# Residual rounds and the gating of the last weights beside the middle chunks of the second products; differences of u from the float32 blocks

## The chip, the core and the metric

One core of one Trainium2 chip runs the whole program. The time is device time of one execution, in microseconds; a kernel's time is the median of its runs. The work is matrix products on TensorE (PE), with VectorE (DVE), ScalarE (ACT) and GpSimd (POOL) preparing operands and taking results, and with DMA transfers, most of them issued from SyncE's queue (SP).

## The reference, cut to what matters

Input x is 1024 tokens of width 1024. Two blocks with adaptive modulation (an even mixer and attention, each followed by an MLP) are followed by a third block with a gated feed-forward network (ffn). The lines that bear on the change:

```
x = layer_norm(ALPHA * x + gate * y, ln_g[layer, 0], ln_b[layer, 0])     # y: the mixer's output
u = x * (1.0 + scale) + shift
y = square(relu(u @ mlp_w1 + mlp_b1)) @ mlp_w2 + mlp_b2                  # 1024 -> 4096 -> 1024
x = layer_norm(ALPHA * x + gate * y, ln_g[layer, 1], ln_b[layer, 1])
...
x = _layernorm(DEEPNORM_ALPHA * x + mix, ln1_g, ln1_b)                   # third block
ffn = (silu(gate half) * value half of conv(x @ w_up)) @ w_down          # 1024 -> 2 x 2816 -> 1024
x = _layernorm(DEEPNORM_ALPHA * x + ffn, ln2_g, ln2_b)
```

The residual of each such pair is ALPHA times the normalised x with the layer norm's scale and bias, plus the bias b2 times the gate in the MLPs. The gate multiplies a whole column of y, so it can be put on the product's result or on the rows of w2.

## The kernel before

All operands of TensorE are pairs of a rounded part and its float32 remainder: ACT casts (`act.copy`), DVE subtracts, and a product is three matmuls (hi x hi, hi x lo, lo x hi). Helpers issue most vector work, so that many instructions stand on one line: `tt` (L305) and `stt` (L308) on DVE, or on POOL when asked; the matmuls all stand on L247.

**Boundary** (`boundary`, L575). Between two parts of the network the last rows of the product before are finished, the rows are normalised into `xres` (z: the normalised rows without scale and bias), and `u_tile` (L567) makes transposed tiles of u: TensorE transposes (L251), ACT writes scale and shift into a float32 tile `uf` (L571), ACT casts it to u's high part (L572), DVE subtracts for the low part. u has two halves of tokens h = 0, 1 and eight tiles of channels. The rows z go to `d_zm` in DRAM.

**First products** (`FmProducts`). u times w1 (or w_up) is done in a scheme with seven products for a 2 x 2 division, instead of eight, on 14 pairs of weight blocks in an MLP and 20 in the ffn. A group is one of the seven, 12 matmuls. It needs differences of blocks: of the weights (`wx`, in part on POOL, and `we`, cast and split), and of u: `diffs` makes the operands `t` for one of four channel positions each time two tiles of the second half are there. It adds u's high and low parts back together (`ur<-u`, on POOL for the first half, on DVE for the second), takes four differences (`tx`, `ur`), casts and splits. Results gather in `rr` (MLP) or `cc` (ffn), the ffn's convolution runs on `cc` and `rr`, and `keep_pair` stores h and its differences (`hx`) in DRAM.

**Residual rounds** (`residual_job`). For each of eight row tiles: load z from `d_zm` into `zt`, `zt` x ALPHA x scale on DVE, + bias row on POOL, store to `d_zm`. The rows stand in `xrow` and `erow`, loaded from POOL's queue. It is a generator; `bg()` runs one step of it at every odd group of the first products.

**Second products** (`second_half`, `TmProducts`). h times w2 goes by the same kind of scheme in chunks of 4, 3, 3, 4 pairs (MLP) or 3, 3, 3 (ffn); a chunk has seven groups g and each group four steps t of 3 matmuls per pair. `he` are the split operands (from `rh`, loads of h, and from `rw`, weights), `beside` and `fetch` make and load them for the groups ahead. Sums go into `acc`, rows of the result, by DVE. In the MLPs the first touch of `acc` is a copy by ACT; in the ffn `acc` is loaded with the residual from `d_zm` ahead. In the last chunk of an MLP `gated_residual` multiplies `acc` by the gate on POOL and adds `zi`, loaded from `d_zm`. The first MLP's second products also carry `ada_side`, the modulation of later parts. The last four pairs of rows of w2 (`wl`) are handled apart, by the boundary after (`last_sums`); since `acc` is already multiplied by then, `wl` is multiplied by the gate: `_Weights.gate` on POOL (L194), `st<-st,gate`, ahead of the split.

**What sets the order.** Each engine runs its instructions in the order of the program. Tiles come from rotating pools: W8 (8 KB a partition, 21 tiles) and T4 (4 KB, 7 tiles: `sf`, `wx`, `rh`, `zt`, `zi`, `uf`, `tx`, `ur`, `gate`, `erow`). SP issues a load once a tile is free, and a store once what it stores is ready; what stands behind waits.

Of the kernel before, what the change touches and what calls it, by code (L numbers as in the profile page):

```python
# [254 lines left out]
def tile_net(ctx: ExitStack, tc: tile.TileContext, x, wts, ada, adag, cols, rows, sfm, rgw, wup, wsp, out):  # L255
# [66 lines left out]
    d_f = drm.tile([16, 4, 1024], F32, name="d_f")  # L322
    d_h = drm.tile([14, 7, 128, 512], F32, name="d_h")
    d_hx = drm.tile([4, 128, 1024], F32, name="d_hx")
    d_zm = drm.tile([1024, 1024], F32, name="d_zm")
# [71 lines left out]

    def last_plan(l, name, first, gate):

        for j in range(4):  # L400
            plan.append({"src": (lambda j=j: d_hx[j]), "mix": ("h", l, j)})
        for j in range(4):
            plan.append({"key": (name, first + j), "dst": lambda: W8("wl")})
            if gate is not None:
                plan[-1]["gate"] = gate

    def mlp_plan(l):
        W(f"w1_{l}", 0, 1, 2, 3)
        last_plan(l, f"w2_{l}", 28, lambda: gate_row.get(2 * l + 1))

# [25 lines left out]
    W("up", 0, 22, 1, 23)  # L436
    last_plan(2, "dn", 18, None)
    ws = _Weights(k, plan)
# [126 lines left out]

    def u_tile(xz, h, kt, uT, G, B, lo=None):
        pb = PB()  # L567
        for j in range(4):
            pe.transpose(pb[:, j * 128:(j + 1) * 128], xz[:, 4 * h + j, kt * 128:(kt + 1) * 128], ident)
        uf = T4("uf")[:, 0:512]  # L570
        act.activation(out=uf, in_=pb, func=AF.Identity, scale=G[:, kt:kt + 1], bias=B[:, kt:kt + 1])  # L571
        act.copy(uT[h][:, 0, kt, :], uf)  # L572
        tt(uT[h][:, 1, kt, :], uf, uT[h][:, 0, kt, :].bitcast(F32), SUB, lo)

    def boundary(hs, wsx, xres, G, B, keys, evacs, spill=None, ops=None):  # L575
# [5 lines left out]
        def residual(t):  # L581

            if spill is not None:
                xr = xres[:, t, :]
                stt(xr, xr, spill[1], rr[0], MUL, MUL)
                tt(xr, xr, rr[1], ADD, None if t % 2 else pool)
                nc.sync.dma_start(out=spill[0][t * 128:(t + 1) * 128, :], in_=xr)
            elif ops is not None:
                nc.sync.dma_start(out=d_zm[t * 128:(t + 1) * 128, :], in_=xres[:, t, :])
        for t in range(8):  # L590
# [4 lines left out]
            for dh in range(2):  # L595
                if t >= 5:
                    for _ in range({(5, 0): 2, (6, 0): 2}.get((t, dh), 1)):
                        u_tile(xres, 0, todo.pop(0), uT, G, B)
                if dh == 0 and norm:
# [26 lines left out]
        for i in (1, 2):  # L626
            w.append(ws.get(keys[i], ahead=0))
            for c, _ in enumerate(fm_mms(pss[i], w[i], uT, 0)):
                if c in (1, 5):
                    residual(2 * i - 2 + c // 4)  # L630
                if (i, c) in ((1, 3), (1, 5), (1, 7), (2, 0), (2, 2), (2, 3), (2, 5), (2, 6)):
                    u_tile(xres, 1, todo.pop(0), uT, G, B)
                    if ops is not None and len(todo) % 2 == 0:
                        diffs(uT, 3 - len(todo) // 2, ops)
        for c, _ in enumerate(fm_mms(pss[0], w[0], uT, 1)):
# [854 lines left out]
    def residual_job(alpha, gname, bname, extra):  # L1490

        if extra is not None:
            load_gate(extra[1])
        gr, cr = xrows(alpha, gname, bname, extra)
        if extra is not None:
            del gate_row[extra[1]]
        yield
        for t in range(8):
# [66 lines left out]
    class Mlp:  # L1565
# [20 lines left out]
        def run(self, uT, jobs=None):  # L1586
# [35 lines left out]

            bgq.append(residual_job(ALPHA, f"lng{2 * l}", f"lnb{2 * l}", (f"b2_{l}", 2 * l + 1)))
# [11 lines left out]
            undefer(9)  # L1635
            return second_half(l, tp, 2 * l + 1, jobs)

# [20 lines left out]

    def second_half(l, tp, gate, jobs=None):

        xres = Rows("acc")
        if gate is None:
            for i in range(4):
                nc.sync.dma_start(out=xres.t[i], in_=d_zm[i * 256:(i + 1) * 256, :].rearrange("(i p) n -> p i n", p=128))
        else:
            load_gate(gate)
            if jobs:
                bgq.append(ada_side(jobs, 1, lambda: st.j in (0, 5, 6)))

        def step(g, t):  # L1670
            c, j = divmod(g, 7)
            st.j = j
            if jobs:
                bg()
# [5 lines left out]
        bg(99)  # L1680
        if gate is not None:
            gated_residual(xres, gate, 1, 0)
        hs, w2 = tail_blocks()
# [590 lines left out]
    def ffn(bargs):  # L2274
# [60 lines left out]

        bgq.append(residual_job(ALPHA2, "ln1g", "ln1b", None))

        def step(p, i):
            undefer()
            if p < fp.n - 1:  # L2340
                if i % 2:
                    bg()
            else:
                begin(tp, i)
# [3 lines left out]
        undefer(9)  # L2348
        return second_half(2, tp, None)

# [94 lines left out]
```

## Time and profile before

| | us |
|---|---|
| median of 3 runs (lowest, highest) | 3838.15 (3836.57, 3841.23) |
| the profiled execution; its span | 3834.72; 3833.0 |
| busy: PE, DVE, ACT, POOL | 3554.3, 2751.7, 1460.0, 715.9 |
| first products: MLP, second MLP, ffn | 293.77, 292.26, 430.10 |
| second products: MLP, second MLP, ffn | 291.99, 291.82, 188.06 |

The profiled execution is one run of the program, recorded by the hardware. A busy TensorE is not yet one at full clock: the granted clock stands beside the busy time of a stretch. A wait in square brackets is the idle time of an engine ahead of an instruction and what ended it.

### The profile page before, as it was taken

The numbers are of one execution on the slowest core, as the hardware profiler recorded it, in microseconds if no ns is written. First come the engines' busy times: TensorE is split into PE (matmuls) and PEld (weight loads), VectorE is DVE, ScalarE is ACT, GpSimd is POOL, SyncE is SP. The second block draws the span as 40 slices with busy tenths as digits, with TensorE's granted clock in tenths as the row PEclk, the third lists the DMA queues.
The fourth block names the chain that finished last, engine by engine and source line by source line (L and its number), as shares of the span: only waits on it lengthen the run. The fifth ranks groups of instructions, "written<-read, shape, count | busy, mean of one in ns | idle before, by whom it ended". The sixth has DMA issues, their size and how long they took to land. (4 is left out here: it accounts for less than half of the span.)

```text
span 3833.0 us, 43642 instructions
## 1 busy us (share of the span) xinstructions
PE 3554.3 (93%) x17098; PEld 2890.7 (75%) x17098; DVE 2751.7 (72%) x3609; ACT 1460.0 (38%) x1924; POOL 715.9 (19%) x473
## 2 busy tenths in 40 slices
PE   7999979999989999999897999998989988899997
PEld 5876767787867788878786778886777766677785
DVE  6565667768897764454556876688889678877787
ACT  4244343344325442353334334432423443344441
POOL 2002133400042000000202441004300034433002
PEclk9999989999999999999899999999989999999998
DMA  6333135465432222100312455344212223322641
GB/s 221 105 132 129 75 118 191 174 231 195 162 122 95 68 79 86 35 34 29 110 72 104 179 181 213 130 165 138 80 57 79 84 82 118 127 99 80 220 150 67
DMA packets 181056, 461.82 MB, mean 120 GB/s; under 512 B 15313, under 2 KB 20065, under 8 KB 180850
## 3 DMA queue, kind: packets, MB, share of 16 engines
q1 hardware_dynamic: 173986, 437.96, 32.3%
q0 software_dynamic: 6864, 21.08, 1.6%
q8 instruction: 134, 2.20, 0.2%
q14 instruction: 72, 0.59, 0.0%
HBM read 337.85 MB, written 121.13 MB: 120 GB/s over the span
## 5 line engine op out<-in xcount | busy, mean ns | idle before, releaser
L247 PE MATMUL ps<-u,wu 128*128 128x512 f32 x2880 | 763.5, 411 | 23.6 <-ACT u L572 14.6
L247 PEld LDWEIGHTS ps<-u,wu 128*128 128x128 f32 x2880 | 538.7, 194 | 152.1 <-ACT u L572 15.8
L247 PE MATMUL ps<-he 128*128 128x512 f32 x2442 | 587.0, 400 | 33.3 <-DVE he L305 24.6
L247 PEld LDWEIGHTS ps<-he 128*128 128x128 f32 x2442 | 465.6, 191 | 147.3 <-DVE he L305 30.7
L247 PE MATMUL ps<-t,we 128*128 128x512 f32 x1728 | 435.6, 402 | 46.4 <-DVE cc L305 31.5
L247 PEld LDWEIGHTS ps<-t,we 128*128 128x128 f32 x1728 | 330.7, 193 | 130.9 <-DVE cc L305 37.1
L247 PE MATMUL pb<-u,we 128*128 128x512 f32 x1152 | 287.0, 398 | 16.1 <-ACT rr L1606 16.1
L247 PE MATMUL ps<-wu,u 128*128 128x256 f32 x1920 | 261.5, 290 | 15.1 <-DVE wu L218 13.0
L247 PEld LDWEIGHTS pb<-u,we 128*128 128x128 f32 x1152 | 219.4, 191 | 69.1 <-ACT rr L1606 18.7
L247 PEld LDWEIGHTS ps<-wu,u 128*128 128x128 f32 x1920 | 242.4, 193 | 25.8 <-DVE wu L218 13.6
L1432 ACT CAST he<-rw 128x1024 fp32r<-128x1024 f32 (+1 forms) x154 | 133.2, 910 | 293.0 <-DVE rw L305 275.9
L305 DVE TENSOR_TENSOR we<-sf,we 128x512 fp32r<-128x512 f32 x192 | 175.7, 926 | 92.4 <-ACT we L1325 90.0
L247 PE MATMUL ps<-pw,wu 128*128 128x512 f32 x816 | 211.0, 407 | 13.8 <-DVE xres L308 7.9
L1904 DVE TENSOR_REDUCE mx<-ps 128x1 f32<-128x128 f32 (+7 forms) x128 | 95.5, 754 | 172.5 <-PE ps L247 172.2
L305 DVE TENSOR_TENSOR acc<-acc,ps 128x1024 f32<-128x1024 f32 (+1 forms) x155 | 162.7, 1050 | 75.1 <-PE ps L247 67.7
L305 DVE TENSOR_TENSOR he<-rw,he 128x1024 fp32r<-128x1024 f32 (+1 forms) x154 | 168.3, 1134 | 45.3 <-ACT he L1432 45.3
L1944 ACT ACTIVATE p<-ps 128x1024 f32<-128x1024 f32 (+7 forms) x128 | 82.9, 649 | 303.5 <-PE ps L247 287.9
L247 PEld LDWEIGHTS ps<-pw,wu 128*128 128x128 f32 x816 | 155.2, 194 | 50.6 <-DVE xres L308 8.4
L305 DVE TENSOR_TENSOR he<-rh,he 128x1024 fp32r<-128x1024 f32 (+1 forms) x154 | 174.4, 1133 | 19.8 <-ACT he L1432 19.8
L1432 ACT CAST he<-rh 128x1024 fp32r<-128x1024 f32 (+1 forms) x154 | 135.5, 910 | 68.7 <-DMA rh<-d_h 37.2
L247 PE MATMUL pb<-he 128*128 128x512 f32 x666 | 159.6, 394 | 0.0
L1325 ACT CAST we<-wx 128x512 fp32r<-128x512 f32 x144 | 84.8, 619 | 188.3 <-POOL wx L305 138.1
(394 smaller groups left out, 6086.0 us busy)
## 6 DMA issues: line engine op xcount, KB each, us to landing
st<-in_wts_dram SPq DMA_DIRECT2D x116, 512.0 KB, 3.3
rh<-d_h SPq DMA_DIRECT2D x105, 512.0 KB, 5.4
sf<-in_wts_dram SPq DMA_DIRECT2D x96, 512.0 KB, 6.9
d_h<-hx SPq DMA_DIRECT2D x37, 1024.0 KB, 4.8
d_h<-rr SPq DMA_DIRECT2D x111, 256.0 KB, 2.3
sta<-in_ada_dram SPq DMA_DIRECT2D x48, 512.0 KB, 3.4
rw<-in_wts_dram SPq DMA_DIRECT2D x28, 768.0 KB, 4.6
sta<-in_adag_dram SPq DMA_DIRECT2D x32, 512.0 KB, 3.9
```

Of the source, the lines that this page charges most:

```text
L247: return self.eng.matmul(out=out, lhsT=lhsT, rhs=rhs, **kw)
L305: (eng or dve).tensor_tensor(out=o, in0=a, in1=b, op=op)
L1325: act.copy(d[:, 0, :], src)
L1432: act.copy(d[:, 0, 0:n, :], src)
L1904: dve.tensor_reduce(out=mx[:, t:t + 1], in_=ps[:, 0:n], axis=AX.X, op=ALU.max)
L1944: act.activation(out=p[:, 128 * i:1024], in_=ps[:, 128 * i:1024], func=AF.Exp)
```

## The change

`diffs` takes its blocks from the float32 tiles that ACT writes: `u_tile` is handed a tile to write, in W8 for the first half and in T4 for the second, and the sums `ur<-u` are no longer made. The casts and subtractions of `t` are four of 512 instead of two of 1024. The rows z go to `d_zm` where each is normalised. The residual rounds move from the first products into the second products, from g = 3 on: a step after every t in the first MLP, where the modulation's side work goes ahead of it, and after every other t elsewhere; what is left is done at the end of the chunk before the last. Both steps of a round are on DVE. The last weights of the MLPs are gated in the same place, by DVE, through DRAM (`d_wl`), and loaded gated in the last chunk. In the ffn `acc` is no longer loaded ahead; its residual is added in the last chunk as in the MLPs, without a gate.

```
-    def u_tile(xz, h, kt, uT, G, B, lo=None):
+    def u_tile(xz, h, kt, uT, G, B, lo=None, uf=None):
-        uf = T4("uf")[:, 0:512]
+        if uf is None:
+            uf = T4("uf")[:, 0:512]
...
             def z(t=t, y=y, nb=nb):
                 act.activation(out=xres[:, t, :], in_=xres[:, t, :], func=AF.Identity, scale=y, bias=nb)
+                if ops is not None:
+                    nc.sync.dma_start(out=d_zm[t * 128:(t + 1) * 128, :], in_=xres[:, t, :])
...
-    def diffs(uT, j, ops):
+    def diffs(b, ops):
-        raw = []
-        for h in range(2):
-            r = T4("ur")
-            for i in range(2):
-                q = uT[h][:, :, j + 4 * i, :]
-                tt(r[:, i * 512:(i + 1) * 512], q[:, 0, :].bitcast(F32), q[:, 1, :].bitcast(F32), ADD, pool if h == 0 else None)
-            raw.append(r)
-        (b11, b21), (b12, b22) = [(r[:, 0:512], r[:, 512:1024]) for r in raw]
+        (b11, b21), (b12, b22) = b
...
-        for d, r in zip(t, (x, raw[0])):
-            f = d.rearrange("p a b c -> p a (b c)")
-            act.copy(f[:, 0, :], r)
-            tt(f[:, 1, :], r, f[:, 0, :].bitcast(F32), SUB)
+        for i, q in enumerate(((x[:, 0:512], x[:, 512:1024]), (b11, b21))):
+            for j in range(2):
+                act.copy(t[i][:, 0, j, :], q[j])
+                tt(t[i][:, 1, j, :], q[j], t[i][:, 0, j, :].bitcast(F32), SUB)
...
             stt(z, z, alpha, gr, MUL, MUL)
-            tt(z, z, cr, ADD, pool)
+            tt(z, z, cr, ADD)
...
-    def gated_residual(xres, gate, th, dh):
+    def add_residual(xres, gate, th, dh):
...
-            tt(x, x, gate_row[gate][:, f].unsqueeze(1).to_broadcast([128, 2, 512]), MUL, pool)
+            if gate is not None:
+                tt(x, x, gate_row[gate][:, f].unsqueeze(1).to_broadcast([128, 2, 512]), MUL, pool)
             tt(x, x, z, ADD)
...
-                if p < fp.n - 1:
-                    if i % 2:
-                        bg()
-                else:
+                if p == fp.n - 1:
                     begin(tp, i)
...
-            for i in range(4):
-                nc.sync.dma_start(out=xres.t[i], in_=d_zm[i * 256:(i + 1) * 256, :].rearrange("(i p) n -> p i n", p=128))
...
+        def gated():
+            for j in range(4):
+                z = T4("zw")
+                nc.sync.dma_start(out=z, in_=wts[_UNITS[f"w2_{l}", 28 + j]])
+                yield
+                tt(z, z, gate_row[gate], MUL)
+                yield
+                nc.sync.dma_start(out=d_wl[j], in_=z)
+                st.written.add(("w", l, j))
+        def work():
             if jobs:
-                bgq.append(ada_side(jobs, 1, lambda: st.j in (0, 5, 6)))
+                yield from ada_side(jobs, 1, lambda: st.j in (0, 5, 6))
+            yield from job
+            if gate is not None:
+                yield from gated()
...
+            if g > 2 and (jobs or t % 2 == 0):
+                next(side_work, None)
             if g >= tp.n - 7:
-                if gate is not None and t == 3 and j in (2, 5, 6):
-                    gated_residual(xres, gate, *((0, 0), (0, 1), (1, 1))[(2, 5, 6).index(j)])
+                if t == 3 and j in (2, 5, 6):
+                    add_residual(xres, gate, *((0, 0), (0, 1), (1, 1))[(2, 5, 6).index(j)])
...
+            elif g == tp.n - 8 and t == 3:
+                run(side_work)
...
-        tp = TmProducts("dn", [[0, 1, 2], [3, 4, 5], [6, 7, 8]], False)
+        tp = TmProducts("dn", [[0, 1, 2], [3, 4, 5], [6, 7, 8]], True)
```

DVE in the ffn's first products, before: one product with a residual round (`zt`); `cc` and `rr` are the convolution's, `we` the weights' splits.

```order
L308 SCALAR_TENSOR_TENSOR rr<-cc,col,rr 128x1022
L305 TENSOR_TENSOR we<-sf,we 128x512
L308 SCALAR_TENSOR_TENSOR zt<-zt,xrow 128x1024
L305 TENSOR_TENSOR we<-sf,we 128x512 x2
L308 SCALAR_TENSOR_TENSOR cc<-cc,col 128x1023
L308 SCALAR_TENSOR_TENSOR cc<-cc,col 128x1022
L305 TENSOR_TENSOR rr<-rr,cc 128x1024
```

The same place after.

```order
L308 SCALAR_TENSOR_TENSOR rr<-cc,col,rr 128x1022
L305 TENSOR_TENSOR we<-sf,we 128x512 x3
L308 SCALAR_TENSOR_TENSOR cc<-cc,col 128x1023
L308 SCALAR_TENSOR_TENSOR cc<-cc,col 128x1022
L305 TENSOR_TENSOR rr<-rr,cc 128x1024
```

The round's step is gone from the product, and so is the addition on POOL that followed it.

DVE in the second MLP's second products, after: from g = 3 on, rounds stand between the splits `he` for the coming group and the sums into `acc`; before, none stood there.

```order
L305 TENSOR_TENSOR erow<-erow,gate 128x1024
L308 SCALAR_TENSOR_TENSOR xrow<-xrow,erow 128x1024
L305 TENSOR_TENSOR he<-rh,he 128x1024 x2
L305 TENSOR_TENSOR he<-rw,he 128x1024 x2
L308 SCALAR_TENSOR_TENSOR zt<-zt,xrow 128x1024
L305 TENSOR_TENSOR zt<-zt,xrow 128x1024
L305 TENSOR_TENSOR he<-rh,he 128x1024
L305 TENSOR_TENSOR acc<-acc,ps 128x2x512
L305 TENSOR_TENSOR he<-rh,he 128x1024
L305 TENSOR_TENSOR acc<-acc,pb 128x512
```

Each round is two steps in DVE's row, ahead of splits that TensorE's next group needs.

DVE in the second MLP's boundary, before: the sums `ur<-u` between the split of two tiles of u and the differences.

```order
L305 TENSOR_TENSOR u_3554<-uf,u_3554 128x512
L305 TENSOR_TENSOR u_3556<-uf,u_3556 128x512
L305 TENSOR_TENSOR ur<-u_3554 128x512
L305 TENSOR_TENSOR ur<-u_3556 128x512
L305 TENSOR_TENSOR tx<-ur 128x512
L305 TENSOR_TENSOR tx<-ur,tx 128x512
L305 TENSOR_TENSOR ur<-ur,tx 128x512
L305 TENSOR_TENSOR ur<-ur 128x512
L305 TENSOR_TENSOR t_3602<-tx,t_3602 128x1024
```

The same place after.

```order
L305 TENSOR_TENSOR u_3557<-ur,u_3557 128x512
L305 TENSOR_TENSOR u_3559<-ur,u_3559 128x512
L305 TENSOR_TENSOR tx<-ur 128x512
L305 TENSOR_TENSOR tx<-ur,tx 128x512
L305 TENSOR_TENSOR ur<-ur,tx 128x512
L305 TENSOR_TENSOR ur<-ur 128x512
L305 TENSOR_TENSOR t_3596<-tx,t_3596 128x512 x2
```

The two sums are gone from DVE's row, and their two partners from POOL's; the first difference follows the splits directly.

## Rows read from the trace of the kernel before

**Rows 1.** Windows of the first products: stretch; busy us per engine; granted clock; DMA.

```profile
533.94:827.71 293.77, 278.69 (x1178) 224.44 (x1176) 213.22 (x232) 102.11 (x169) 96.17 (x61) 0.98 0.52 186
...
2087.50:2379.76 292.26, 276.36 (x1177) 222.68 (x1176) 213.43 (x232) 102.23 (x169) 96.63 (x61) 0.98 0.53 187
...
3142.80:3572.90 430.10, 398.56 (x1681) 319.30 (x1680) 351.45 (x346) 186.19 (x279) 147.54 (x85) 0.97 0.32 118
```

**Rows 2.** Timeline of PE, first MLP: start us, us, instruction, [idle before <-releaser].

```profile
533.94 2.89 PE L247 MATMUL ps<-u,we 128*128 128x512 f32 x12
...
547.70 2.96 PE L247 MATMUL pb<-u,we 128*128 128x512 f32 x12
```

**Rows 3.** Waits of PE, 3110 to 3360: us in total, times, longest.

```profile
PE ps L247 <- DVE cc L305: 29.0, 8, 5.7
```

**Rows 4.** Waits of PE, 3360 to 3560.

```profile
PE ps L247 <- DVE cc L305: 2.5, 4, 0.6
```

**Rows 5.** Timeline of all engines, an ffn product with a round.

```profile
3237.38 1.22 DVE L308 SCALAR_TENSOR_TENSOR zt<-zt,xrow 128x1024 f32<-128x1024 f32 x1
...
3238.67 2.79 POOL L305 TENSOR_TENSOR zt<-zt,xrow 128x1024 f32<-128x1024 f32 x1 [9.87 <-DVE zt L308]
...
3241.94 4.54 DVE L308 SCALAR_TENSOR_TENSOR cc<-cc,col 128x1023 f32<-128x1023 f32 x2
...
3255.38 1.22 PE L247 MATMUL ps<-t,we 128*128 128x512 f32 x2 [5.67 <-DVE cc L305]
```

**Rows 6.** Timeline, an ffn product without a round.

```profile
3461.47 2.60 DVE L308 SCALAR_TENSOR_TENSOR cc<-cc,col 128x1023 f32<-128x1023 f32 x2 [0.45 <-ACT cc L2283]
```

**Rows 7.** Timeline, the head of the first MLP's first products.

```profile
551.85 1.23 DVE L305 TENSOR_TENSOR erow<-erow,gate 128x1024 f32<-128x1024 f32 x1 [9.71 <-issue]
...
557.61 5.29 PE L247 MATMUL ps<-t,we 128*128 128x512 f32 x12 [6.94 <-DVE rr L305]
```

**Rows 8.** Timeline, one cycle of the first MLP's boundary.

```profile
482.63 0.77 ACT L571 ACTIVATE uf<-pb,gb 128x512 f32<-128x512 f32 x1
...
483.43 0.62 ACT L572 CAST u<-uf 128x512 fp32r<-128x512 f32 x1
...
486.02 2.38 DVE L305 TENSOR_TENSOR ur<-u 128x512 f32<-128x512 f32 x2
486.18 3.33 POOL L305 TENSOR_TENSOR ur<-u 128x512 f32<-128x512 f32 x2 [7.21 <-DVE u L305]
...
490.82 1.04 ACT L1260 CAST t<-tx 128x1024 fp32r<-128x1024 f32 x1 [5.44 <-DVE tx L305]
...
493.16 0.77 ACT L571 ACTIVATE uf<-pb,gb 128x512 f32<-128x512 f32 x1
```

**Rows 9.** Waits of PE, 440 to 520, the first MLP's boundary.

```profile
PE pb L251 <- ACT uf L571: 11.2, 2, 5.7
```

**Rows 10.** Timeline, the start of the ffn's second products.

```profile
3589.80 1.22 DVE L305 TENSOR_TENSOR acc<-acc,ps 128x1024 f32<-128x1024 f32 x1 [5.07 <-DMA acc<-d_zm]
```

**Rows 11.** Timeline, the last chunk of the second MLP.

```profile
2604.89 3.35 POOL L194 TENSOR_TENSOR st<-st,gate 128x1024 f32<-128x1024 f32 x1
2605.93 3.40 DVE L305 TENSOR_TENSOR he<-rh,he 128x1024 fp32r<-128x1024 f32 x1
...
2610.39 1.21 DVE L218 TENSOR_TENSOR wu<-st,wu 128x1024 fp32r<-128x1024 f32 x1
2611.52 1.21 DVE L305 TENSOR_TENSOR he<-rh,he 128x1024 fp32r<-128x1024 f32 x1
```

**Rows 12.** Waits of PE, 2600 to 2720.

```profile
PE ps L247 <- DVE he L305: 10.8, 6, 2.9
```

**Rows 13.** Windows of the second MLP's middle chunks.

```profile
2480.00:2520.00 40.00, 40.00 (x175) 32.49 (x174) 31.53 (x34) 12.88 (x17) 0.00 (x0) 1.00 0.42 138
2520.00:2560.00 40.00, 40.00 (x175) 32.62 (x174) 34.74 (x36) 14.76 (x19) 0.00 (x0) 1.00 0.60 217
```

**Rows 14.** DMA issues of the page: KB each, median us to landing.

```profile
zt<-d_zm SPq DMA_DIRECT2D x24, 512.0 KB, 6.9
```

More of the change, by code (lines that the diff above doesn't have):

```diff
@@ L323, in tile_net @@
     d_h = drm.tile([14, 7, 128, 512], F32, name="d_h")
+    d_wl = drm.tile([4, 128, 1024], F32, name="d_wl")
     d_hx = drm.tile([4, 128, 1024], F32, name="d_hx")
@@ L396, in part, with last_plan @@
         plan.extend(mm + ww if p == 0 and layer < 2 else ww + mm)
-    def last_plan(l, name, first, gate):
+    def last_plan(l, name, first, gated):
         for j in range(4):
@@ L402, in last_plan @@
         for j in range(4):
-            plan.append({"key": (name, first + j), "dst": lambda: W8("wl")})
-            if gate is not None:
-                plan[-1]["gate"] = gate
+            d = {"dst": lambda: W8("wl")}
+            if gated:
+                d.update({"src": (lambda j=j: d_wl[j]), "mix": ("w", l, j)})
+            else:
+                d["key"] = (name, first + j)
+            plan.append(d)
     def mlp_plan(l):
         W(f"w1_{l}", 0, 1, 2, 3)
-        last_plan(l, f"w2_{l}", 28, lambda: gate_row.get(2 * l + 1))
+        last_plan(l, f"w2_{l}", 28, True)
     W("e_fm", 0, 2, 1, 3)
@@ L436, in tile_net @@
     W("up", 0, 22, 1, 23)
-    last_plan(2, "dn", 18, None)
+    last_plan(2, "dn", 18, False)
     ws = _Weights(k, plan)
@@ L587, in residual, with raw @@
                 nc.sync.dma_start(out=spill[0][t * 128:(t + 1) * 128, :], in_=xr)
-            elif ops is not None:
-                nc.sync.dma_start(out=d_zm[t * 128:(t + 1) * 128, :], in_=xres[:, t, :])
+        def raw(h, kt):
+            if ops is None:
+                return None
+            i, j = divmod(kt, 4)
+            if (h, kt) not in raws:
+                if h == 0:
+                    w_ = W8("ur", (128, 2, 2, 512), F32)
+                    raws.update({(0, 4 * a + j + b): w_[:, b, a, :] for a in range(2) for b in range(2)})
+                else:
+                    w_ = T4("ur")
+                    raws.update({(1, 4 * a + j): w_[:, a * 512:(a + 1) * 512] for a in range(2)})
+            return raws[h, kt]
+        raws = {}
         for t in range(8):
@@ L597, in boundary @@
                     for _ in range({(5, 0): 2, (6, 0): 2}.get((t, dh), 1)):
-                        u_tile(xres, 0, todo.pop(0), uT, G, B)
+                        kt = todo.pop(0)
+                        u_tile(xres, 0, kt, uT, G, B, uf=raw(0, kt))
                 if dh == 0 and norm:
@@ L631, in boundary @@
                 if (i, c) in ((1, 3), (1, 5), (1, 7), (2, 0), (2, 2), (2, 3), (2, 5), (2, 6)):
-                    u_tile(xres, 1, todo.pop(0), uT, G, B)
-                    if ops is not None and len(todo) % 2 == 0:
-                        diffs(uT, 3 - len(todo) // 2, ops)
+                    kt = todo.pop(0)
+                    u_tile(xres, 1, kt, uT, G, B, uf=raw(1, kt))
+                    if kt > 3 and ops is not None:
+                        diffs([[raws[h, kt - 4 + 4 * a] for a in range(2)] for h in range(2)], ops)
         for c, _ in enumerate(fm_mms(pss[0], w[0], uT, 1)):
@@ L1657, in begin, with second_half @@
             tp.sums(2)
-    def second_half(l, tp, gate, jobs=None):
+    def second_half(l, tp, gate, job, jobs=None):
         xres = Rows("acc")
-        if gate is None:
-            for i in range(4):
-                nc.sync.dma_start(out=xres.t[i], in_=d_zm[i * 256:(i + 1) * 256, :].rearrange("(i p) n -> p i n", p=128))
-        else:
+        if gate is not None:
             load_gate(gate)
-            if jobs:
-                bgq.append(ada_side(jobs, 1, lambda: st.j in (0, 5, 6)))
+        def gated():
[8 more added lines that the diff above has]
+        def work():
+            if jobs:
+                yield from ada_side(jobs, 1, lambda: st.j in (0, 5, 6))
+            yield from job
+            if gate is not None:
+                yield from gated()
+        side_work = work()
         def step(g, t):
@@ L1672, in step @@
             st.j = j
-            if jobs:
-                bg()
+            if g > 2 and (jobs or t % 2 == 0):
+                next(side_work, None)
             if g >= tp.n - 7:
-                if gate is not None and t == 3 and j in (2, 5, 6):
-                    gated_residual(xres, gate, *((0, 0), (0, 1), (1, 1))[(2, 5, 6).index(j)])
+                if t == 3 and j in (2, 5, 6):
+                    add_residual(xres, gate, *((0, 0), (0, 1), (1, 1))[(2, 5, 6).index(j)])
                 ws.split(min(ws.ng + 8, max(ws.ns, ws.ng + (4 * j + t) // 3)))
+            elif g == tp.n - 8 and t == 3:
+                run(side_work)
         tp.run(xres, step)
-        bg(99)
-        if gate is not None:
-            gated_residual(xres, gate, 1, 0)
+        add_residual(xres, gate, 1, 0)
         hs, w2 = tail_blocks()
@@ L2334, in evac @@
                 defer(2, lambda: value_part(f, cc[:, 1, :], cc[:, 0, :]))
-        bgq.append(residual_job(ALPHA2, "ln1g", "ln1b", None))
         def step(p, i):
             undefer()
[L2340 to L2343, printed above, removed]
+            if p == fp.n - 1:
                 begin(tp, i)
@@ L2348, in ffn @@
         undefer(9)
-        return second_half(2, tp, None)
+        return second_half(2, tp, None, residual_job(ALPHA2, "ln1g", "ln1b", None))
     def finish(hs, wsx, xres):
```

7 lines of the change are left out of this document (1 added, 6 removed).

## The prediction

> **What bounds the kernel now.** TensorE is the longest engine, but its matmuls are the same before and after, in the same order, so the time can only change by what it loses between them. I read the loss stage by stage. The windows of the three stages of first products come first [rows 1]: 293.77, 292.26 and 430.10 us. In a stretch without stalls a group of 12 matmuls starts 2.75 us after the one before: five groups lie between 533.94 and 547.70 [rows 2]. A stage of 14 pairs has 98 groups, 98 x 2.75 = 269.5 us; the ffn has 140, 385.0 us. So these stages lose 24.3, 22.8 and 45.1 us.
>
> The waits of TensorE say where. Over the part of the ffn in which the residual rounds run, it waits 29.0 us in 8 stalls for `cc` on DVE [rows 3]; over the part after the last round, 2.5 us [rows 4]. Eight stalls, eight rounds. The timeline of one round shows the mechanism: the `zt` step costs DVE 1.22 us, but the addition that follows on POOL takes 2.79, and with it POOL's own `wx` sums come later, beside the next pair of `cc` steps, which take 4.54 us [rows 5] where the same pair takes 2.60 without a round [rows 6]. TensorE then idles 5.67 us. In the first MLP one more stall stands at the head: DVE sits 9.71 us before `erow`, and behind that wait stands the `rr` step for which TensorE idles 6.94; the 12 matmuls after it take 5.29 us, since the granted clock falls when it idles [rows 7].
>
> Then the boundaries: DVE and ACT, not TensorE, set the cycle in which two transposed tiles become one pair of operands t. From one `uf` to the same one a cycle later it is 493.16 - 482.63 = 10.53 us [rows 8], and TensorE waits for `uf` twice, 11.2 us in all, at each of three boundaries [rows 9].
>
> **Boundaries.** The sums `ur<-u` go: 2 on DVE (2.38 us) and 2 on POOL (3.33 us) per cycle. They stand in a row: `tx` needs POOL's, which end at 486.18 + 3.33 = 489.51, while DVE had its last `u` difference by 486.02 and could begin `tx` then. So 3.5 us leave the chain of a cycle; casting t in four halves instead of two wholes gives back some 0.4 us of ACT overhead (4 x 0.62 - 2 x 1.04). 3.1 us x 3 cycles x 3 boundaries = 28. Bounds: -33 if the stall's clock loss goes with it, -15 if `uf`, held longer in its new tile, or TensorE's transposes become next in line. The stores `d_zm<-xres` go out earlier on SP; what stands behind them there are weights that are asked for long ahead: nothing, 0 to +2.
>
> **First products.** All 24 rounds leave. In the ffn the stretch after the rounds still waits 2.5 us in 200 [rows 4], which makes 385 + 5 = 390; the head of the stage, where the last operands come late, may keep 4 more. Gain 430 - 394 = 36. For the MLPs the same stall is gone but a few waits for ACT may stay: 22 and 21 of the 24.3 and 22.8. Together -79. Bounds: -60 (a quarter of the stalls has another cause) to -80.
>
> **Start of the ffn's second half.** The four loads of `acc` leave. DVE waits 5.07 us for them [rows 10], with TensorE's next operands behind it in its order, and the `rh` loads stand behind them on SP's queue. -9, bounds -5 (the row alone) to -11. Its eight first additions become copies on ACT; eight others come with `zi` in the last chunk, where DVE also has the last weights to split: 8 x 1.13 = 9 us of DVE, of which I let 5 show. Bounds 0 to +10.
>
> **Last chunks of the MLPs.** Four POOL multiplications by the gate leave each. One takes 3.35 us, and a DVE `he` step beside it 3.40 instead of 1.21; TensorE waits 10.8 us for `he` there [rows 11, 12]. 4 x 2.2 = 8.8 us of DVE: -9 for the first, -10 for the second. Bounds 0 to -14 each. The eight POOL multiplications of `acc` stay.
>
> **Middle chunks.** What arrives there, per MLP: 8 rounds of two DVE steps, 2 x 1.13 us (a step of 1024 elements begins 1.13 us after the one ahead of it, 2610.39 to 2611.52 [rows 11]), two steps on `erow` and `xrow`, and four on the weights: 8 x 2.26 + 2.26 + 4 x 1.13 = 24.9 us. Nothing runs on POOL there (0.00 busy), so no step is stretched. In the same place DVE is busy 31.53 to 34.74 us of 40 [rows 13], so 5.3 to 8.5 us of 40 are free. A step is 9 matmuls, 2.07 us. In the second MLP and the ffn a round comes every six steps, 12.4 us: 7.3 us per 40. That about fits: +5 each, bounds 0 to +12. In the first MLP the side work on the modulation goes first, and the rounds come one every three steps, 6.2 us: 14.6 us per 40 against 5.3 free, so 9.3 per 40 too much, over the 50 us of eight rounds 11.6; the four weights and the wait for `erow` add some 4. +16, bounds +10 to +30.
> Each round also brings a load and a store on SP. The load of the next round goes out when the store before it has, which waits for DVE; a landing takes 6.9 us [rows 14] and DVE stands in order, with `he` (for which TensorE waits) behind `zt`. At a round every 12.4 us the load has landed; at 6.2 us it has not, by about 1 us, and that is within the +10 to +30. `rh` loads stand behind the store on SP, one group and more ahead of their use: 0.
>
> The Trainium skill, "Perfetto Trace Analysis", section "Optimizing Scalar/DVE Operations", speaks against this part: where DVE is saturated, some of its work may go to ScalarE or GpSimd, and the change moves work from GpSimd to DVE, in chunks where DVE is 79 to 87% busy. The same section adds that the two share a read port, so that moving between them may not help, and rows 5 and 6 (4.54 against 2.60) agree with that half. Taken by its first half alone the result is the first rival below.
>
> **Sum.** -28 - 79 - 9 + 5 - 19 + 26 = -104. The profiled execution took 3834.72 us (span 3833.0), so 3730.7; the median of the runs is 3.4 above the profiled one: 3734.
>
> **Rivals.** (a) *DVE becomes the bound of the second products.* Its idle time there turns out not to be usable, because it lies in front of waits for TensorE's sums, and each added step goes through in full: 25 + 25 + 20 = 70 instead of 26, so 3734 + 44 = 3778. For it: 34.74 of 40 busy [rows 13], and the steps stand ahead of `he` in DVE's order. Against it: TensorE was busy 40.00 of 40 with those same 34.74, so DVE is ahead there, not level.
> (b) *The stalls of the first products are not the rounds'.* If POOL's own `wx` sums alone stretch `cc`, the stalls stay, and only the rest is gained: 3734 + 79 = 3813. Against it: rows 4, where the `wx` sums still run and 2.5 us are left.
> (c) *Slower: DVE in order behind each load of a round.* If SP sends the load of a round only just ahead of DVE's step (no free tile of that pool earlier, or stores in the way), DVE waits for the whole landing, with `he` and so TensorE behind it. All else sums to -130; with the 70 us of steps exposed too, 60 remain, and 24 rounds eat them at 2.5 us of wait each: from there the kernel is slower. At the full 6.9 us it is 24 x 6.9 = 166, so 3838 - 130 + 70 + 166 = 3944. For it: the 9.71 us wait before `erow` is of this kind [rows 7]. Against it: that was a load at the head of a burst; the `zt` step in rows 5 began without idle time before it.
>
> **How the numbers follow.** Forecast 0.78, (a) 0.13, (b) 0.05, (c) 0.04. The bounds of the terms, taken together without all falling on one side, give the forecast 3705 to 3770; adding (a) the range is 3705 to 3780. A difference under 0.2% (7.7 us) can't be told from none. Forecast, (a) and (b) are faster; (c) is slower; a case halfway between (a) and (c) is all that gives the same: faster 0.95, same 0.01, slower 0.04.
>
> **What would show it.** In the profile after: windows of the first products of 270 to 273, 270 to 273 and 393 to 396 us, with no wait for `cc` over 0.7 us; cycles of the boundary near 7.4 us and waits for `uf` under 3 us each; no `acc<-d_zm`; `he` steps at 1.2 us beside fewer POOL spans in the last chunks. In the middle chunks of the first MLP, waits of TensorE for `he` of 10 to 30 us together; in the other two, few. The prediction is wrong if the waits for `he` there reach 60 us (a), if DVE shows idle time ending in a DMA ahead of `zt` (c), or if `cc` stays at 4.5 us (b).

## The result

The changed kernel takes 3733.88 us (median; 3732.42 to 3738.05) where the kernel before, on the same chip, takes 3837.45: a ratio of 0.973, 95% interval 0.9713 to 0.9747. The profiled execution has a span of 3736.3 us, 96.7 less than before.

Windows of the changed kernel: first products of the first MLP, second products, the same for the second MLP and for the ffn. After the stretch come its length, the busy time of PE, PEld, DVE, ACT and POOL with the count of instructions, the granted clock, the DMA share and GB/s.

```profile
523.99:795.11 271.12, 271.12 (x1178) 220.81 (x1176) 179.72 (x222) 102.04 (x169) 69.74 (x50) 1.00 0.46 163
795.11:1104.20 309.09, 287.77 (x1209) 228.68 (x1208) 266.66 (x259) 111.06 (x128) 22.05 (x10) 0.97 0.64 218
2060.49:2331.85 271.36, 271.36 (x1178) 220.90 (x1177) 179.25 (x222) 102.05 (x169) 69.61 (x50) 1.00 0.46 163
2331.85:2617.48 285.63, 276.37 (x1178) 222.44 (x1176) 243.10 (x216) 110.68 (x127) 21.13 (x10) 0.98 0.59 205
3074.18:3471.15 396.97, 390.51 (x1682) 314.53 (x1680) 311.45 (x337) 184.86 (x279) 111.99 (x75) 1.00 0.29 104
3471.15:3664.38 193.23, 181.33 (x757) 143.41 (x756) 166.42 (x166) 79.08 (x100) 2.15 (x4) 0.98 0.61 214
```

The first products of the MLPs now have TensorE busy in all of 271.12 and 271.36 us, at a granted clock of 1.00; the ffn's take 396.97 [rows 1]. The second products went another way in each part: the first MLP's 291.99 to 309.09, the second's 291.82 to 285.63, the ffn's 188.06 to 193.23.

Waits of TensorE in the changed kernel, first in the ffn's first products, then in the first MLP's boundary (total us, times, longest):

```profile
PE ps L247 <- DVE cc L305: 5.4, 8, 0.7
...
PE pb L251 <- ACT ur L576: 4.8, 2, 2.4
```

Eight waits for `cc` of up to 5.7 us have become eight of up to 0.7 [rows 3]; the two for the transposed tile, 11.2 us together [rows 9], are 4.8.

To see inside the second products, chunks are told apart by their matmuls: 336 in a chunk of four pairs, 252 in one of three; a chunk ends where so many have started, to half a microsecond. In the first MLP only the matmuls on `he` are counted: the side work on the modulation adds 32 small ones (`pb<-ones,aacc`) to the first two chunks, which belong to no pair. The expectations recorded below counted them too, so their cuts after the first chunk lie 8 to 9 us earlier: where they speak of 78.5 and 95.6 us for the third and last chunk of the changed kernel, it is 79.9 and 86.4 here. Without a stall a chunk takes 77.0 or 57.8 us. All terms of the profiled pair:

| | before | after | difference | forecast |
|---|---|---|---|---|
| boundaries, end of the part ahead to the first group | 72.1, 71.6, 71.2 | 58.8, 58.8, 59.0 | -38.4 | -28 |
| first products | 293.8, 292.3, 430.1 | 271.1, 271.4, 397.0 | -76.7 | -79 |
| ffn's second products, first chunk | 71.0 | 63.2 | -7.8 | -9 |
| last chunks of the MLPs | 92.0, 98.4 | 86.4, 89.0 | -15.0 | -19 |
| last chunk of the ffn | 58.9 | 68.6 | +9.7 | +5 |
| first MLP, chunks one to three | 79.9, 62.1, 58.0 | 79.7, 63.1, 79.9 | +22.7 | +16 |
| second MLP, chunks one to three | 77.0, 58.4, 58.0 | 77.0, 61.5, 58.1 | +3.2 | +5 |
| ffn, middle chunk | 58.2 | 61.4 | +3.2 | +5 |
| all else | | | +2.4 | 0 |

Most of "all else" is 3.4 us ahead of the first boundary, where nothing was changed; the boundary's start lies between 461.3 and 466.1 us in the kernels below as well, so this is the difference of one execution from another. It may also be why the profiled execution (3738.05) is 4 us above its own median; the other executions have no trace to show it.

### The profile page after: what moved, and what is told of

Same layout as the page of the kernel before. It is cut to its first block, busy times and chain, and to the rows that moved or that the text cites. A ratio compares the mean times of both kernels' runs of the same rounds, so it can differ in the third digit from the quotient of the medians.

```text
span 3736.3 us, 43621 instructions
## 1 busy us (share of the span) xinstructions
PE 3532.5 (95%) x17098; PEld 2874.1 (77%) x17098; DVE 2661.7 (71%) x3640; ACT 1471.2 (39%) x1957; POOL 559.3 (15%) x415
## 5 line engine op out<-in xcount | busy, mean ns | idle before, releaser
L247 PE MATMUL ps<-t,we 128*128 128x512 f32 x1728 | 423.7, 394 | 6.5 <-DVE cc L305 5.4
L1926 DVE TENSOR_REDUCE mx<-ps 128x1 f32<-128x128 f32 (+7 forms) x128 | 95.6, 755 | 174.9 <-PE ps L247 174.6
L305 DVE TENSOR_TENSOR we<-sf,we 128x512 fp32r<-128x512 f32 x192 | 143.4, 757 | 97.9 <-ACT we L1341 96.2
L305 DVE TENSOR_TENSOR we<-wx,we 128x512 fp32r<-128x512 f32 x144 | 144.2, 1003 | 52.8 <-ACT we L1341 52.8
L305 DVE TENSOR_TENSOR he<-rh,he 128x1024 fp32r<-128x1024 f32 (+1 forms) x154 | 165.8, 1078 | 19.2 <-ACT he L1448 19.1
L305 DVE TENSOR_TENSOR acc<-acc,ps 128x1024 f32<-128x1024 f32 (+1 forms) x148 | 153.9, 1040 | 14.8 <-PE ps L247 14.5
```

Source lines behind the costliest of these rows:

```text
L247: return self.eng.matmul(out=out, lhsT=lhsT, rhs=rhs, **kw)
L305: (eng or dve).tensor_tensor(out=o, in0=a, in1=b, op=op)
L1926: dve.tensor_reduce(out=mx[:, t:t + 1], in_=ps[:, 0:n], axis=AX.X, op=ALU.max)
```

## Experiments

### The boundaries alone

```
 kernel before, with the new u_tile, raw and diffs; nothing else moved
```

> The kernel before with the boundaries alone changed: differences of u from the float32 tiles, nothing moved. Theory (the sums ur<-u were the chain of a boundary): each of the three stretches from the end of one part to the first group of the first products gets 9 to 14 us shorter, waits of PE for uf fall from 11 to about 5 us, first and second products stay at 294, 292, 430 and 292, 292, 188 us; in all 30 to 38 us less than the kernel before. Rival (part of what the boundaries gained in the changed kernel came from the stores d_zm<-xres, which are sent earlier there): 15 to 25 us less.

Measured: 3805.48 us against 3834.89 before on the same chip, ratio 0.9923 (0.9909 to 0.9938), 29 us, just under the 30 to 38 expected. In the profile the three boundaries are 36.9 us shorter together (58.8, 58.8 and 60.4 us), while the first products take 5.5 us more in all (295.0, 295.7, 430.9); the second products take 293.0, 288.6 and 188.0. The windows of the first boundary, of the kernel before and of this one:

```profile
461.85:533.94 72.09, 55.49 (x225) 43.88 (x224) 47.96 (x66) 31.65 (x38) 22.70 (x16) 0.86 0.20 74
```
```profile
462.95:521.74 58.79, 52.19 (x226) 41.16 (x225) 36.45 (x63) 32.18 (x46) 12.18 (x9) 0.94 0.26 90
```

The boundary is 13.3 us shorter for 225 to 226 matmuls; 9.9 to 10 us of that is idle time (72.09 - 55.49 = 16.6, against 6.6), and 3.3 is the matmuls themselves, at a mean granted clock of 0.94 instead of 0.86. The sums were the chain; the rival (the earlier stores) is out, since the stores stand in their old place here and the boundary is as short as in the changed kernel. In the timeline of the changed kernel the cycle reads 489.17 - 481.96 = 7.21 us instead of 10.53 [rows 8], with `tx` directly behind the splits:

```profile
481.96 0.77 ACT L576 ACTIVATE ur<-pb,gb 128x512 f32<-128x512 f32 x1
...
485.35 0.68 DVE L305 TENSOR_TENSOR tx<-ur 128x512 f32<-128x512 f32 x1
...
489.17 0.77 ACT L576 ACTIVATE ur<-pb,gb 128x512 f32<-128x512 f32 x1
```

### Rounds on DVE, in the first products

```
-            tt(z, z, cr, ADD, pool)      # kernel before
+            tt(z, z, cr, ADD)
```

> The kernel before with the addition of each residual round on DVE instead of POOL, still in the first products. Theory (the stalls come from POOL's addition, which stretches DVE's steps and delays POOL's own sums wx): cc pairs take 2.6 us again, the ffn's first products fall from 430 to 405 to 415, the MLPs' from 294 and 292 to 276 to 284, in all 30 to 50 us less than the kernel before. Rival (the stalls come from a round's place in DVE's order and its length there, which grows by 1.13 us): the same time or up to 15 us more, with waits for cc as long as before.

Measured: 3791.67 us against 3834.89, ratio 0.9891 (0.9874 to 0.9907). The first products take 281.5, 280.8 and 412.2 us. DVE in an ffn product with a round, and TensorE's waits over the part of the ffn's first products in which the rounds run (3117 to 3360 us):

```profile
3206.57 1.22 DVE L308 SCALAR_TENSOR_TENSOR zt<-zt,xrow 128x1024 f32<-128x1024 f32 x1
3207.82 1.23 DVE L305 TENSOR_TENSOR zt<-zt,xrow 128x1024 f32<-128x1024 f32 x1
3208.97 1.28 DVE L305 TENSOR_TENSOR we<-sf,we 128x512 fp32r<-128x512 f32 x2
3210.17 2.60 DVE L308 SCALAR_TENSOR_TENSOR cc<-cc,col 128x1023 f32<-128x1023 f32 x2
```
```profile
PE ps L247 <- DVE cc L305: 11.0, 8, 1.9
```

One more step stands in DVE's order, yet the `cc` pair takes 2.60 us, not 4.54 [rows 5], and the eight waits are at most 1.9 us. So POOL's addition, through the steps of DVE beside it and POOL's own sums behind it, made most of the stall, 18 of the 29.0 us [rows 3]; the 11.0 that are left, against 5.4 in the whole stage without rounds, stay with rounds that are wholly on DVE. About half of what the changed kernel gains in the first products (41.6 of 76.7 us) comes from that one word. In the MLPs what is left is the wait at the head, 7.3 and 8.1 us here, and the slow matmuls behind it; in the ffn, rounds on DVE still cost 15.2 us (412.2 against 397.0).

### Gating back on POOL

```
+            d["key"] = (name, first + j)
+            if gated:
+                d["gate"] = lambda: gate_row.get(2 * l + 1)
-            if gate is not None:
-                yield from gated()
```

> The changed kernel with the gating of the last MLP weights back on POOL in the last chunks, and not in the middle chunks. Theory (POOL's multiplications stretch DVE's he steps there): last chunks back from 95.6 and 89.0 to 99 and 98 us, the third chunk of the first MLP 2 to 4 us shorter; in all 5 to 11 us more than the changed kernel. Rival (the last chunks got shorter for another reason, such as the residual's order of loads): 3 to 6 us less than the changed kernel.

Measured: 3750.46 us, ratio to before 0.978 (0.9765 to 0.9794); the changed kernel has 0.973. Last chunks 92.8 and 98.0 us (86.4 and 89.0 in the changed kernel), the third chunk of the first MLP 76.3 (79.9). The `he` steps beside POOL are long again in the second MLP's last chunk:

```profile
2593.95 3.42 DVE L305 TENSOR_TENSOR he<-rh,he 128x1024 fp32r<-128x1024 f32 x1
```

The theory holds: 6.4 and 9.0 us of last chunk for 3.6 us of middle chunk. In all the medians lie 16.6 us apart, where 5 to 11 were expected; these three chunks account for 11.8 of it, and where the rest lies wasn't found. In the changed kernel the first MLP's last two `zw` steps stand at the end of that third chunk and wait 2.69 and 1.05 us for their loads.

### The addition of a round on POOL, in the second products

```
-            tt(z, z, cr, ADD)            # changed kernel
+            tt(z, z, cr, ADD, pool)
```

> The changed kernel with the addition of each residual round on POOL, in the second products. Theory (a POOL addition of 2.4 us costs DVE about 2.2 us in steps that run beside it, more than the 1.13 us that it saves DVE): second products longer, 10 to 40 us more than the changed kernel in all, he steps of 2 to 3.4 us in the middle chunks. Rival (DVE is saturated in the middle chunks, and what is taken from it is gained): 8 to 20 us less, most of it in the third chunk of the first MLP (78.5 us now).

Measured: 3757.05 us, ratio 0.9798 (0.9784 to 0.9813). Most of the loss is in the third chunk of the first MLP: 94.7 us instead of 79.9, 14.7 of the 19.3 us between the two profiled executions. Its window, then DVE, its waits and SP's queue there:

```profile
936.32:1030.97 94.65, 67.71 (x253) 51.39 (x252) 68.41 (x58) 23.14 (x28) 22.26 (x7) 0.89 0.61 215
```
```profile
956.95 1.22 DVE L308 SCALAR_TENSOR_TENSOR zt<-zt,xrow 128x1024 f32<-128x1024 f32 x1 [2.90 <-DMA zt<-d_zm]
958.09 3.96 DVE L305 TENSOR_TENSOR he<-rw,he 128x1024 fp32r<-128x1024 f32 x2
```
```profile
DVE zt L308 <- DMA zt<-d_zm: 19.3, 7, 5.2
...
SPq L1518 <- POOL zt L305: 32.2, 7, 5.2
SPq L1518 <- DMA zt<-d_zm: 26.2, 7, 5.8
```

DVE is busy 68.41 us, no less than with the addition on DVE (66.85 in the changed kernel), though it has eight steps fewer: the `he` pair beside POOL takes 3.96 us instead of 1.82. And the round became longer from load to store, so SP waits for POOL, and DVE up to 5.2 us for the next load, 19.3 us in all against 7.5. The Trainium skill, "Perfetto Trace Analysis", section "Optimizing Scalar/DVE Operations", has both halves of this: a saturated DVE may be relieved by GpSimd, but the two share a read port, so it might not help. The run agrees with the second half: 3.96 us against 1.82 beside POOL, and no DVE time gained. That the port is the reason no run here shows.

### What the third chunk of the first MLP pays for

```
 changed kernel, first MLP only
+            if dma or t == 0:      # load        (dma=False: one load, one store, 16 steps)
+            if steps or t == 0:    # stt, tt     (steps=False: 8 loads, 8 stores, 2 steps)
+            if dma or t == 7:      # store
```

> The changed kernel with the residual rounds of the first MLP doing their 16 DVE steps, but with one load ahead of the first and one store behind the last instead of eight of each; the residual of that MLP is then not the reference's. It asks what the third chunk of the first MLP's second products (78.5 us now, 57.8 without stalls) pays for. Theory D (DVE has too little free time for the steps): 70 to 78 us. Theory S (each store waits for DVE on SP's queue, and the loads of rh behind it come late): 60 to 66 us.

> The changed kernel with the eight loads and stores of the first MLP's residual rounds, but with the two DVE steps in the first round alone (the residual is not the reference's). Theory D: the third chunk takes 58 to 63 us. Theory S: 66 to 76 us, since a store still waits on SP for its load to land, with rh behind it.

Measured: 3728.95 and 3728.34 us, ratios 0.9713 (0.9698 to 0.9729) and 0.9709 (0.9694 to 0.9725). The third chunk's windows: of the kernel before, of the changed kernel, of steps without DMA and of DMA without steps:

```profile
969.70:1027.74 58.04, 58.04 (x254) 47.38 (x252) 49.26 (x49) 23.15 (x29) 0.00 (x0) 1.00 0.51 178
```
```profile
937.86:1017.79 79.93, 66.72 (x254) 51.02 (x252) 66.85 (x66) 22.95 (x28) 0.00 (x0) 0.91 0.72 250
```
```profile
938.31:1010.59 72.28, 62.77 (x253) 49.12 (x252) 65.89 (x65) 21.07 (x26) 0.00 (x0) 0.95 0.52 177
```
```profile
935.28:1003.28 68.00, 60.91 (x254) 49.00 (x252) 50.94 (x52) 23.25 (x28) 0.00 (x0) 0.95 0.86 294
```

58.0, 79.9, 72.3 and 68.0 us. With the rounds wholly elsewhere (next experiment) it is 62.7, of which the gating is nearly all (57.9 when that is moved too). So of some 22 us above 57.8 the gating has 5, the steps alone add 9.5, the transfers alone 5.3, and the two together 2.4 more than their sum. For TensorE the 22 us are 13.2 of idle time (7.0 before `acc`, 6.0 before `he`) and 8.7 of slower matmuls, 66.72 us busy at a mean granted clock of 0.91 against 58.04 at 1.00. Both theories were half right. D names the larger part: DVE is busy 65.9 of 72.3 us with the steps alone. S names a part that the prediction put at nothing; in the changed kernel TensorE, SP's queue, ACT and DVE wait like this in the same chunk (total us, times, longest):

```profile
PE ps L247 <- DVE acc L305: 7.0, 2, 3.6
PE ps L247 <- DVE he L305: 6.0, 4, 3.2
...
SPq L1518 <- DMA zt<-d_zm: 24.4, 6, 5.9
...
SPq L1518 <- DVE zt L305: 17.9, 7, 2.7
...
ACT he L1448 <- DMA rh<-d_h: 36.0, 8, 9.2
...
DVE zt L308 <- DMA zt<-d_zm: 7.5, 6, 2.3
```

L1518 is the store of a round. SP stands before it for 42 of 80 us, longer for the round's load to land than for DVE; the loads of `rh` stand behind it, and ACT waits 36.0 us for them. With the transfers alone ACT waits 35.9 us for `rh`, with the steps alone 7.3, without rounds 9.7: the transfers make that wait. The split is by chunks of one profiled execution each; the same chunk varied by 2 to 3 us between kernels in which it is the same (79.9 and 82.7), and by the medians either run gains only some 5 us on the changed kernel.

### The first MLP's rounds, and both MLPs' rounds, in the first products

```
 changed kernel
+            if l == 0:                       # l < 2 for both
+                bgq.append(job)              # rounds beside the first products, both steps on DVE
+                job = iter(())
+                elif i % 2:
+                    bg()
 residual_job: xrow and erow asked for, three steps later used
```

> The changed kernel with the first MLP's residual rounds back in its first products, both steps on DVE, and with the rows (xrow, erow) asked for three steps ahead of their use. Theory (a round on DVE alone has room there, and the 7 us stall at the head was the wait for erow): first products 272 to 276 us (271.1 now), third chunk 59 to 63 us (78.5 now), in all 12 to 18 us less than the changed kernel. Rival (the rounds cost as much there as in the kernel before with its addition on DVE, 281.5): first products 279 to 283, in all 3 to 8 us less.

> The same for both MLPs. Theory: the second MLP gains nothing by it, since its rounds in the middle chunks cost 3 us: within 4 us of the kernel with the first MLP's alone. Rival (rounds in the first products cost nothing at all): 3 us less than that kernel.

Measured: 3717.71 us, ratio 0.9683 (0.9667 to 0.9698), and 3714.23 us, ratio 0.9677 (0.9658 to 0.9697). First products of the first MLP and third chunk in the first of the two:

```profile
522.19:793.45 271.26, 271.26 (x1177) 220.97 (x1176) 212.27 (x240) 102.32 (x169) 83.80 (x53) 1.00 0.56 201
```
```profile
934.95:997.70 62.75, 60.47 (x254) 48.22 (x252) 52.44 (x53) 24.76 (x31) 0.00 (x0) 0.97 0.67 232
```

With the rounds, the first products take 271.26 us, against 271.12 without: on DVE alone they cost nothing there, although DVE is busy 212.27 us of it, and the stall at the head was the wait for `erow`. The 16 us by the medians came from the third chunk (79.9 to 62.7). For the second MLP the chunk that had the rounds fell from 61.5 to 58.1, and its first products stayed at 271.4, so by chunks the rival was right (nothing at all); the two medians lie too close to tell.

### The ffn's last chunk

```
 changed kernel
+                if gate is not None and t == 3 and j in (2, 5, 6):
+        if gate is not None:
             add_residual(xres, gate, 1, 0)
```

> The changed kernel without the residual of the ffn in its last chunk: the loads zi and the eight additions are left out, so the output lacks that residual. It asks what the last chunk of the ffn's second products (68.6 us now, 58.9 in the kernel before) pays for. Theory (the eight additions, 9 us of DVE, fall on a DVE with no free time): 58 to 61 us, in all 7 to 11 us less than the changed kernel. Rival (a wait for zi or the later split of the last weights): 63 to 68 us.

Measured: 3732.56 us, ratio 0.9725 (0.971 to 0.9739), which the runs don't tell from the changed kernel's 0.973. The last chunk takes 63.7 us; its window, and that of the changed kernel:

```profile
3593.87:3657.60 63.73, 60.96 (x254) 48.42 (x254) 56.02 (x56) 23.52 (x29) 1.05 (x2) 0.97 0.48 166
```
```profile
3595.80:3664.38 68.58, 61.77 (x255) 48.32 (x254) 60.66 (x60) 23.61 (x29) 1.05 (x2) 0.98 0.63 215
```

4.9 of the 10.8 us above 57.8 go with the loads and additions; 5.9 stay, in the range of the rival, though not for its reasons. The kernel before had 58.9 in this chunk. The trace of this run shows what is new there: seven of the ffn's rounds are done step by step from g = 3 on, and the eighth, left over, is done in one go at the end of the middle chunk. Its load goes out on SP just ahead of its step:

```profile
3592.39 0.73 SPq L1513 DMA_DIRECT2D zt<-d_zm  x1
...
3597.95 1.23 DVE L308 SCALAR_TENSOR_TENSOR zt<-zt,xrow 128x1024 f32<-128x1024 f32 x1 [2.39 <-DMA zt<-d_zm]
...
3614.06 5.98 PE L247 MATMUL ps<-he 128*128 128x512 f32 x18 [2.25 <-DVE acc L305]
```

DVE waits 2.39 us for the load, TensorE then 2.25 us for a sum into `acc`, and the 18 matmuls behind that take 5.98 us where 18 take 4.3 in the rest of the chunk. With TensorE's only other wait there, 0.35 us, that is 4.3 of the 5.9 us. The changed kernel has the same two waits, 2.80 and 2.39 us. That they would go with the eighth round is read from the trace; no run here moved it.

### Loads two steps early, gating in the first products, and both

```
+                    if t == 1:
+                        early[q] = load_residual(*q)      # zi, before: at t == 3, ahead of its addition
+                    elif t == 3:
+                        add_residual(xres, gate, *q, early.pop(q))
...
+            bgq.append(both())                            # rounds, then the four zw, in the first products
```

> The kernel with both MLPs' rounds in the first products, and the loads zi of the last chunks issued two steps ahead of the additions. Theory (DVE stands 6 to 8 us before zi in the second MLP's last chunk, with he behind): that chunk 82 to 86 us (88.1 now), the first MLP's 88 to 91, in all 3 to 7 us less. Rival (no tile is free any earlier, so that SP waits instead and the loads behind come late): the same or up to 5 us more.

> The kernel with both MLPs' rounds in the first products, and the gating of the last weights behind them there. Theory (DVE has room in the first products, and in the third chunk of the first MLP the gating alone costs 4 to 5 us): that chunk 58 to 59 us (62.4 now), first products as now (271.3), in all 3 to 6 us less. Rival (the gate row and zw take tiles that the weights sf need): first products 274 to 282 us, no gain.

> Rounds and gating of both MLPs in their first products on DVE, and the loads zi two steps early. Theory (the two gains are in different places: 4 to 5 us in the third chunk of the first MLP, 4 us in the last chunk of the second MLP, 3 us in the ffn's last): both stay, 8 to 12 us less than the kernel with the rounds alone moved (3714 us), so 3702 to 3706. Rival (what the gating took from the middle chunks comes back as two more us in the three stages of first products and as later loads of the last weights): 3707 to 3712.

Measured: 3706.10 us, ratio 0.9661 (0.9643 to 0.9679); 3712.41 us, ratio 0.9674 (0.9659 to 0.9688); and both 3703.30 us, ratio 0.9643 (0.9627 to 0.9658). The second MLP's last chunk with both MLPs' rounds moved, and with the loads early as well, and DVE's waits for `zi` in either:

```profile
2503.14:2591.24 88.10, 80.50 (x339) 64.21 (x338) 77.32 (x57) 27.59 (x28) 19.39 (x7) 0.96 0.47 146
...
DVE acc L305 <- DMA zi<-d_zm: 7.9, 3, 4.1
```
```profile
2500.87:2584.70 83.83, 80.37 (x339) 64.14 (x339) 77.13 (x57) 27.50 (x28) 20.29 (x7) 0.98 0.48 157
...
DVE acc L305 <- DMA zi<-d_zm: 2.2, 1, 2.2
```

Early loads take 4.3 us from that chunk and 3 from the ffn's last (69.5 to 66.4); the first MLP's last chunk hardly moves (82.9 to 82.2). Gating in the first products takes the third chunk of the first MLP from 62.6 to 57.9, as expected, but the three stages of first products grow by 1.3, 0.4 and 1.8 us (only two of them hold gating), and the median is 1.8 us lower where 3 to 6 were expected, too little to tell. With both, the gains stand together by chunks (57.9 for that third chunk, 82.3 for the second MLP's last). The median, 3703 us, is the lowest here and 0.8% below the changed kernel's, but its runs (3696 to 3709) overlap with those of the early loads alone (3702 to 3715). In it the second products read:

```profile
797.15:1081.85 284.70, 279.34 (x1209) 226.38 (x1208) 241.36 (x237) 110.56 (x128) 20.30 (x7) 0.99 0.56 187
2308.03:2583.59 275.56, 272.00 (x1177) 220.70 (x1176) 219.34 (x194) 110.28 (x127) 19.39 (x7) 1.00 0.48 162
3436.72:3626.06 189.34, 179.72 (x758) 142.23 (x757) 166.13 (x166) 78.99 (x100) 2.15 (x4) 0.99 0.63 218
```

284.70, 275.56 and 189.34 us, where 269.5, 269.5 and 173.3 would be without a stall. What is left sits in the last chunks (83.8, 82.3 and 66.5), in the ffn's other two, and in the first MLP also in the first two (79.7 and 63.4), beside the side work on the modulation.

## Why the prediction was right

The forecast was 3734 us and the median is 3733.88; that they agree so closely is luck. On the profiled pair the forecast was -104 and the difference -96.7, with errors of both signs in the terms.

- **First products, -79 against -76.7.** Right, and for the reason given: rows 5 and 6 showed POOL's addition stretching the `cc` pair, and with the addition on DVE the pair was 2.60 us at once. The MLPs came out as counted (-22.6, -20.9); the ffn kept 3 us more than forecast, with eight waits of up to 0.7 us for `cc`.
- **Boundaries, -28 against -38.4, outside the bound of -33.** The chain was right: 7.21 us a cycle where 7.4 was worked out, so 9.9 us of idle time left each boundary where 9.3 was forecast. The failed step is the bound: it allowed 5 us in all for the clock, and the matmuls of the first boundary alone took 3.4 us less (55.49 us busy before, 52.07 after, at 0.86 and 0.94 of the clock). Here a stall costs its idle time and then slow matmuls, and both go together.
- **Last chunks of the MLPs, -19 against -15.0.** Right in mechanism by the run that put the gating back (6.4 and 9.0 us), and in size for the second MLP (-9.4 against -10). Too large for the first (-5.6 against -9): the forecast took the waits of the second MLP [rows 12] for both, and in the first MLP's last chunk (1028 to 1120 us) the kernel before waits only this for `he`:

```profile
PE ps L247 <- DVE he L305: 5.9, 3, 2.9
```

- **First MLP's middle chunks, +16 against +22.7, inside 10 to 30.** The steps of DVE were costed near what they cost alone (forecast 11.6; measured 9.5, plus 5 for the gating, forecast 4 with `erow`). The failed step is "`rh` loads stand behind the store on SP, one group and more ahead of their use: 0": the store waits for its round's load to land and for DVE and keeps SP from the loads, and ACT waits for `rh`. Transfers and the interaction with the steps are 7.7 us. The sign named for it, 10 to 30 us of TensorE waiting for `he`, came as 6.0 for `he` and 7.0 for `acc`; the rest of the loss is the slower clock, which that sign did not count.
- **Second MLP and ffn, +5 each, against +3.2 each.** The argument by free time per 40 us [rows 13] held at a round every 12.4 us. Waits of SP and ACT by themselves are no price: over the second MLP's second and third chunks SP stands 48 us before the stores of the rounds and ACT waits 23.0 us for `rh`, and TensorE waits 1.6 us in all.
- **ffn's last chunk, +5 against +9.7; its first chunk, -9 against -7.8.** Of 9 us of additions 4.9 showed, as forecast. The failed step behind the rest is "at a round every 12.4 us the load has landed": the last of the eight rounds has no such spacing, DVE stands 2.80 us before its load in the changed kernel, and TensorE behind DVE. That is what rival (c) describes, in one round out of eight.
- **The rivals.** (a) would have needed 70 us in the second products; 29.1 came in the middle chunks. (b) fell with the windows of 271 us. (c) was real in kind, so that its sign did show: in the first MLP DVE waited up to 2.3 us for a `zt` load, 7.5 us in six waits, and 2.8 us once in the ffn; that is far under the 2.5 us for each of 24 that the price needed.

## What to carry to other kernels

A stall is worth its idle time plus the matmuls run at a lower granted clock behind it, where there are any (in the changed kernel's last ffn chunk a wait of 2.39 us has them, one of 2.37 us has none); read both from the window's busy time, not from the list of waits alone. Before moving side work to a quieter place, ask what made it dear where it was: here half of the loss was that it ran on POOL beside DVE, and rounds wholly on DVE cost nothing in the MLPs' first products, which they were moved out of (in the ffn's, 15 us were left). A load, step and store per round on one in-order queue holds every load behind the store until the round's own load has landed and its step is done; spread the rounds, the last one too, ask early, and count what stands behind the store. Before matmuls are counted to cut a stage into parts, leave out those of other work that runs beside it.

## What the hardware showed that was not expected

- Eight rounds of two DVE steps cost 0.1 us in the first MLP's first products, in which DVE is busy 78% of the time (212.27 of 271.26 us), and the same eight cost 17 us in the third chunk of the first MLP's second products, where it is busy 84% even without them (52.44 of 62.75 us). The rounds also come closer there, one in 8.6 us against one in 19.1, so no run tells how much of the difference is spacing and how much DVE's free time.
- Taking eight steps of 1.13 us from DVE and giving them to POOL left DVE's busy time where it was (68.41 against 66.85 us), and made the chunk 15 us longer.
